# The first stage of a hybrid attention and state-space layer: x in half rows, the root's table fetched early, 1/rms taken with the scale, and another order of the first projection

## The chip, the cores and the metric

The program runs on one core of a Trainium2 chip. The metric is the time of one execution in device microseconds (us), as the median of the runs that are shown. The engines are TensorE (PE, with its weight loads as PEld), VectorE (DVE), ScalarE (ACT), GpSimd (POOL) and SyncE (SP), which issues the DMAs.

## What is computed

One layer of a diffusion backbone, in float32. Its first step is what matters here: the 512 rows of x are divided by their root mean square, scaled and shifted per column by two vectors that come from a matrix product with w_mod (the modulation), and multiplied by the columns of w_in. Seven blocks of 128 of these columns, called z, are made in the first stage; attention, the scan, the output projection and a last RMSNorm follow.

```python
shift, scale, gate = jnp.split((jax.nn.silu(c) @ w_mod + b_mod)[:, None, :], 3, axis=-1)
shift_c, scale_c, gate_c = jnp.split(jax.nn.silu(c_ctx) @ w_mod + b_mod, 3, axis=-1)
px = (rmsnorm(x, norm_g) * (1 + scale) + shift) @ w_in
pc = (rmsnorm(ctx, norm_g) * (1 + scale_c) + shift_c) @ w_in
...
y = xf * lax.rsqrt(jnp.mean(xf * xf, axis=-1, keepdims=True) + EPS)
```

## The kernel before, in words

Activations are held transposed: 16 blocks of 128 columns of x (`KT = 16`, index `j` or `k`), each a tile of 128 partitions by 512 tokens. For products in float32 quality each activation and each weight is split in a high part (a rounded copy, made by ScalarE) and a low part (what is left, made by a subtraction on VectorE or GpSimd), and every product is three matmuls: high by high, high by low, low by high.

**Loading x** (`load_latent`, lines 131 to 164). x comes in four column quarters, two DMAs each, with runs of 2 KB. For each quarter ScalarE squares the four token tiles with a sum along the row (line 145), and TensorE transposes 128 by 128 pieces into PSUM banks (line 150), four to a block. The block is copied out by VectorE, or by ScalarE for the last of each quarter (lines 151 to 154). Then the sums are reduced and scaled on VectorE (lines 155 and 103), the root is taken on ScalarE (line 104), which needs another activation table, its reciprocal and four diagonal matrices are made on VectorE (lines 105 and 160), TensorE spreads 1/rms over all partitions with them (line 161), and ScalarE copies the result to `rsb` (line 163).

**The blocks** (lines 216 to 254). For each block `j` four DMAs of 512 KB bring w_mod (`wm`, seven buffers), and 32 narrow matmuls make `md`, in four column groups of the array. ScalarE copies it (`mds`), four small matmuls sum the groups (`ms`), and VectorE adds the biases and makes `mv` (lines 241 and 242). `md` and `ms` lie in the one PSUM bank of tag `pv`, so the next block's `md` can't begin before VectorE has read `ms`. With `mv`, VectorE makes `full` from the normalised block (line 245), ScalarE the high part `xh` (line 247), VectorE the low part `xl` (line 249) and then the next block times 1/rms (`norm_x`, line 200). A DMA of 448 KB brings the weights of z (`wr`, three buffers; `wsr` in the trace), ScalarE casts them to `wh`, and GpSimd makes `wl` (lines 228 to 233). `z_part(j, us)` is the 21 z matmuls of a block, or some of them; those of block `j - 1` are put into block `j`: twelve between `md` and `ms`, nine behind `ms`.

**Order.** A planner lays out each engine's queue before the run: it goes through its own model of time, and gives each engine, of the instructions that are ready in it, the one that stands first in the code. On the chip each queue runs in that order. `keep_in_program_order` (all matmuls made with `mmo`, and `norm_x`) pins an instruction behind the one traced before it on its engine. `md` of block 0 is thus pinned behind the matmuls that spread 1/rms. SP's queue issues all DMAs here, in its own order, and waits there for a free buffer.

After the last block come the context's activations, v and dt (lines 255 to 394), and the rest of the layer.

Of the kernel before, what the change touches and what calls it, by code (L numbers as in the profile page):

```python
# [6 lines left out]
F32 = mybir.dt.float32  # L7
# [29 lines left out]
# columns of the packed constants  # L37
C_ID, C_SEL, C_AP, C_AN, C_TRI, C_TRIT, C_MF, C_MB, C_END = 0, 128, 130, 258, 386, 514, 642, 770, 898
# columns of the packed small parameters
# [4 lines left out]
def emit(tc, xin, ctxT, wmod, wgate, bgate, wz, wvd, wu, wo, fng, vecs, cst, rope, out, dbg=None):  # L44
# [15 lines left out]
    def f32(ap):  # L60
        return ap.bitcast(F32)

    with es:
# [12 lines left out]
        nc.sync.dma_start(c_sb, cst[:, 0:P + 2])  # L76
# [6 lines left out]
        identb = pc.tile([P, P], BF16, name="identb")  # L83
        nc.vector.tensor_copy(identb, ident)
# [3 lines left out]
        # persistent activations: transposed normalised inputs in two exact parts  # L88
        cy = es.enter_context(tc.tile_pool(name="cy", bufs=1))
        px_s = es.enter_context(ExitStack())  # L90
        px = px_s.enter_context(tc.tile_pool(name="px", bufs=1, side="right"))
        xh = [px.tile([P, S], F32R, tag=f"xh{k}", name=f"xh{k}") for k in range(KT)]
# [14 lines left out]
        def silu2(src, o, tmp):  # L107
            """o = 2 * src * sigmoid(src) = src * (1 + tanh(src / 2))"""
            nc.scalar.activation(tmp, src, AF.Tanh, scale=0.5)
            nc.vector.scalar_tensor_tensor(out=o, in0=tmp, scalar=1.0, in1=src, op0=ALU.add, op1=ALU.mult)  # L110

# [4 lines left out]
        def rms_rows(o, acc, n, tag):  # L116
            """1 / rms of every token, on all partitions, from the sums of squares per partition."""
# [13 lines left out]
        def load_latent():  # L131
            """Latent tokens: transposed as they come, in column blocks; 1 / rms of every token on all partitions."""
            xtags = ["mm", "sa", "tp", "mm", "sa", "tp", "mm"]
            ssq = sp.tile([P, NT, 4], F32, tag="ssq", name="ssq_x")
            rs = sp.tile([P, NT], F32, tag="rs", name="rs_x")
            xin_v = xin.rearrange("(t p) d -> p t d", p=P)
            for q in range(4):
                xt = []
                for h2 in range(2):
                    x_ = cy.tile([P, 2, 512], F32, tag=f"{('ca', 'cb')[h2]}{q}", name=f"xt_{q}_{h2}")  # L140
                    nc.sync.dma_start(x_, xin_v[:, 2 * h2:2 * h2 + 2, q * 512:(q + 1) * 512])
                    xt += [x_[:, 0, :], x_[:, 1, :]]
                for t in range(NT):
                    junk = sp.tile([P, 512], BF16, tag="stmp", name=f"junk_{q}_{t}")
                    nc.scalar.activation(junk, xt[t], AF.Square, accum_out=ssq[:, t, q:q + 1])
                for i in range(4):
                    k = 4 * q + i
                    tps = bank(xtags[k % 7], f"xT_{k}")
                    for t in range(NT):
                        nc.tensor.transpose(tps[:, t * P:(t + 1) * P], xt[t][:, i * P:(i + 1) * P], ident)  # L150
                    if i == 3:
                        nc.scalar.activation(xr[k], tps, AF.Copy)
                    else:
                        nc.vector.tensor_copy(xr[k], tps)
# [22 lines left out]
        # silu of the two modulation vectors, zero-padded to one column group  # L177
# [21 lines left out]
        def norm_x(j):  # L199
            tc.keep_in_program_order(nc.vector.tensor_tensor(out=xr[j], in0=xr[j], in1=rsb, op=ALU.mult))  # L200

        norm_x(0)

# [12 lines left out]
        for j in range(KT):  # L216
            mt = bank("pv", f"md_{j}", shape=(P, 260))
# [15 lines left out]
            tt(nc.gpsimd, wl, wr, f32(wh), ALU.subtract)  # L233
            wzs.append((wh, wl))
            if j > 0:
                z_part(j - 1, range(0, 4))
# [8 lines left out]
            nc.vector.tensor_scalar(out=full, in0=xr[j], scalar1=mv[:, 2:3], scalar2=mv[:, 0:1],  # L245
                                    op0=ALU.mult, op1=ALU.add)
            nc.scalar.activation(xh[j], full, AF.Copy)
            lo = px.tile([P, S], F32R, tag=f"xl{j}", name=f"xl{j}")
            tt(nc.vector, lo, full, f32(xh[j]), ALU.subtract)
            xl.append(lo)  # L250
            if j + 1 < KT:
                norm_x(j + 1)
            if j > 0:
                z_part(j - 1, range(4, NZ))
# [19 lines left out]
        def gate_step(ld):  # L274
            """One k block of 512 gate columns: products per partition, summed over partitions after the last."""
# [22 lines left out]
        def load_unit(u, ctxp=False):  # L298
            """Yields (k, hi, lo) weight blocks [128, 128] of unit u."""
# [110 lines left out]
        # dt: softplus(u) = max(u,0) + log1p(exp(-|u|)), log1p(e) = 2 atanh(e / (2 + e))  # L410
# [48 lines left out]
        def conv_silu(pa, pb, ci, o):  # L459
            """Depthwise conv of width 3 and silu: pa [128, n] in PSUM -> o in SBUF."""  # L460
# [13 lines left out]
        def ssd_group(g, units):  # L474
# [65 lines left out]
            for pr in range(2):  # L540
                tix = 2 * g + pr
                # state term of both heads at once: exp(cs) scales it afterwards
# [10 lines left out]
                for hh in range(2):  # L553
# [3 lines left out]
                    for d in range(2):  # L557
                        # the row of running sums on all partitions; the differences take its place
# [451 lines left out]
```

## Time and profile before

| | us |
|---|---|
| median of three runs | 1057.65 |
| lowest and highest | 1056.16 and 1060.71 |
| span of the profiled execution | 1054.8 |
| TensorE busy in it | 1009.6 (96%) |
| VectorE busy | 722.0 (68%) |
| ScalarE busy | 494.6 (47%) |
| GpSimd busy | 173.5 (16%) |

The share of an engine is an average over the whole span. Rows of the timeline give a start in us from the span's start, a duration, the engine, the line of the kernel, the operation, its output and inputs by the program's names with their shapes, how many were merged in the row, and in brackets how long the engine had been idle before it and what released it. A matmul's duration includes its way through the array, so that rows of matmuls that follow each other overlap; the distance between their starts is what each costs. The granted clock (PEclk) is 1.00 at TensorE's upper level of 2.4 GHz and 0.50 at the lower one of 1.2.

### The profile page before, as it was taken

To read this page: it belongs to the slowest core of one execution; us is meant where nothing else is said; L and a number is where in the kernel's file an instruction comes from. 1 tells how busy PE (TensorE), PEld (TensorE's weight loads), DVE (VectorE), ACT (ScalarE), POOL (GpSimd) and SP (SyncE) were. 2 spreads that over 40 slices of the span, in tenths; PEclk is the share of its full clock that TensorE was granted. 3 is DMA by queue.
4 is the path that set the end of the run, shared out by engine and by line. 5 is a ranking of instruction groups with operands and counts; after the bars stand their busy time and mean duration, and the time that the engine had idled before them with its cause. 6 is when DMAs were issued, how large, how long until landed. Compare 5 with 4: busy or idle time off the path is not lost.

```text
span 1054.8 us, 15524 instructions
## 1 busy us (share of the span) xinstructions
PE 1009.6 (96%) x5682; PEld 818.7 (78%) x5682; DVE 722.0 (68%) x1474; ACT 494.6 (47%) x1064; POOL 173.5 (16%) x120
## 2 busy tenths in 40 slices
PE   5999999999999989989989999999999998999996
PEld 4677789788778868868868777777777777888885
DVE  4332378585875985885889888788798866333765
ACT  6222275263352453263345567666666655333333
POOL 1232200000210110110037100000000008744220
PEclk9999999999999999989999999999999999999998
DMA  9999963354244244444331211112111135442304
GB/s 333 385 347 348 343 212 95 110 165 147 70 120 145 92 149 125 112 120 139 120 107 56 84 61 42 59 40 80 41 40 61 61 99 221 151 167 91 100 33 160
DMA packets 50845, 143.25 MB, mean 136 GB/s; under 512 B 5544, under 2 KB 5928, under 8 KB 50512
## 3 DMA queue, kind: packets, MB, share of 16 engines
q1 hardware_dynamic: 50768, 142.25, 40.5%
q8 instruction: 45, 0.74, 0.3%
q14 instruction: 32, 0.26, 0.1%
HBM read 137.96 MB, written 4.27 MB: 135 GB/s over the span
## 4 chain that ended last, share of the span: by engine, by line
PE 61%; DVE 12%; DMA 5%; ACT 3%; issue 3%; POOL 1%; SPq 0%; ACTq 0%; DVEq 0%; POOLq 0%
PE pj L49 25%; PE o L49 14%; PE pjc L49 5%; PE pv L49 3%; PE ptp L756 3%; PE sl L49 3%; DMA wg<-in_wgate_dram 2%; PE vps L49 2%; DVE df L566 2%; DVE wl L55 2%; DMA df<-csd 2%; PE sc L49 2%; DVE ga L290 1%; DVE df L575 1%; PE stx L49 1%
## 5 line engine op out<-in xcount | busy, mean ns | idle before, releaser
L49 PE MATMUL pj<-xh,wh 128*128 128x512 f32 x560 | 225.5, 403 | 0.0
L49 PE MATMUL pj<-xl,wh 128*128 128x512 f32 x560 | 224.6, 401 | 0.0
L49 PE MATMUL pj<-xh,wl 128*128 128x512 f32 x560 | 224.0, 400 | 0.0
L308 ACT ACTIVATE wh<-wr 128x512 fp32r<-128x512 f32 x140 | 87.9, 630 | 137.5 <-PE pjc L49 66.2
L49 PEld LDWEIGHTS pj<-xh,wl 128*128 128x128 f32 x560 | 105.7, 189 | 21.3 <-issue 0.9
L55 DVE TENSOR_TENSOR wl<-wr,wh 128x512 fp32r<-128x512 f32 x140 | 103.5, 742 | 24.9 <-ACT wh L308 21.0
L49 PEld LDWEIGHTS pj<-xl,wh 128*128 128x128 f32 x560 | 106.4, 190 | 15.1 <-issue 1.9
L49 PEld LDWEIGHTS pj<-xh,wh 128*128 128x128 f32 x560 | 106.5, 190 | 13.9 <-issue 1.0
L55 DVE TENSOR_TENSOR wol<-wo,woh 128x512 fp32r<-128x512 f32 x56 | 53.3, 968 | 63.6 <-ACT woh L846 57.3
L290 DVE SCALAR_TENSOR_TENSOR ga<-wg,sc,ga 128x512 f32<-128x512 f32 x64 | 50.8, 794 | 49.2 <-DMA wg<-in_wgate_dram 48.1
L55 POOL TENSOR_TENSOR ec<-ec,ec 128x512 f32<-128x512 f32 x8 | 11.2, 1397 | 349.2 <-DVE ec L55 328.9
L846 ACT ACTIVATE woh<-wo 128x512 fp32r<-128x512 f32 x56 | 34.8, 630 | 70.8 <-PE o L49 62.3
L55 POOL TENSOR_TENSOR hacc<-hacc,hsq 128x512 f32<-128x512 f32 x14 | 20.4, 1454 | 288.7 <-ACT hsq L654 286.3
L49 PE MATMUL pjc<-chq,wh 128*128 128x256 f32 x224 | 65.2, 291 | 2.1 <-DVE xs L468 2.1
L49 PE MATMUL pjc<-clq,wh 128*128 128x256 f32 x224 | 64.4, 288 | 0.0
L49 PE MATMUL pjc<-chq,wl 128*128 128x256 f32 x224 | 63.7, 284 | 0.0
L760 ACT ACTIVATE ph<-ptp 128x512 fp32r<-128x512 f32 x72 | 41.1, 597 | 28.2 <-PE ptp L756 26.8
L49 PE MATMUL o<-woh,hsh 128*128 128x512 f32 x128 | 50.9, 397 | 3.1 <-ACT part L865 3.1
L55 DVE TENSOR_TENSOR pl<-ptp,ph 128x512 fp32r<-128x512 f32 x72 | 48.4, 683 | 7.8 <-ACT ph L760 7.4
L566 DVE SCALAR_TENSOR_TENSOR df<-df,cs,cs_sb 128x128 f32<-128x128 f32 x128 | 48.3, 433 | 4.6 <-ACT ec L563 4.5
L49 PEld LDWEIGHTS pjc<-chq,wh 128*128 128x128 f32 x224 | 42.2, 189 | 11.5 <-ACT ec L563 1.6
L55 POOL TENSOR_TENSOR wsl<-wsr,wsh 128x896 fp32r<-128x896 f32 x16 | 33.9, 2116 | 101.0 <-ACT wsh L231 95.7
(282 smaller groups left out, 2341.8 us busy)
## 6 DMA issues: line engine op xcount, KB each, us to landing
wr<-in_wu_dram SPq DMA_DIRECT2D x70, 512.0 KB, 3.9
wm<-in_wmod_dram SPq DMA_DIRECT2D x64, 512.0 KB, 7.5
wg<-in_wgate_dram SPq DMA_DIRECT2D x64, 256.0 KB, 2.6
wo<-in_wo_dram SPq DMA_DIRECT2D x32, 512.0 KB, 4.5
df<-csd SPq DMA_DIRECT2D x32, 256.0 KB, 4.1
wsr<-in_wz_dram SPq DMA_DIRECT2D x16, 448.0 KB, 6.6
wr_v<-in_wvd_dram SPq DMA_DIRECT2D x16, 288.0 KB, 2.9
xt<-in_xin_dram SPq DMA_DIRECT2D x8, 512.0 KB, 7.5
```

The lines of the kernel that those rows point to most:

```text
L49: return nc.tensor.matmul(o, l, r, start=start, stop=stop)
L55: eng.tensor_tensor(out=o, in0=a, in1=b, op=op)
L290: geng.scalar_tensor_tensor(out=ga, in0=wg, scalar=sc0[:, k:k + 1], in1=ga, op0=ALU.mult, op1=ALU.add)
L308: nc.scalar.activation(wh, rr, AF.Copy)
L566: nc.vector.scalar_tensor_tensor(out=df[:, cc], in0=bc[:, cc], scalar=cs[:, d, c, r:r + 1], in1=mF if d == 0 else mB, op0=ALU.subtract, op ...
L575: nc.vector.scalar_tensor_tensor(out=dx[0][:, cc], in0=df[:, cc], scalar=dtt[:, d, c, r:r + 1], in1=dx[0][:, cc], op0=ALU.mult, op1=ALU.add)
L756: nc.tensor.transpose(tp[:, i * P:(i + 1) * P], pt[i][:, n * P:(n + 1) * P], ident)
L760: nc.scalar.activation(ph, tp, AF.Copy)
L846: nc.scalar.activation(wh, wr[:, i, :], AF.Copy)
```

## The change

- x comes in two column halves of four DMAs each, one for every token tile, with runs of 4 KB; the constants' DMA goes behind the first two. Each tile is squared at once over 1024 columns, eight squares in all. VectorE copies every transposed block.
- A root of one element stands ahead of the squares, so that its table is fetched there.
- `norm_x` is gone. `full` is the block times the scale times 1/rms, the shift goes into the making of the high part (as a bias) and of the low part.
- The low part of z's weights is made by VectorE.
- Four of block 0's seven groups of z products (twelve matmuls) go ahead of the modulation of block one, two groups between it and its sums, one behind.

Only comments differ elsewhere.

```diff
-        nc.sync.dma_start(c_sb, cst[:, 0:P + 2])
...
+        xt = [[cy.tile([P, 1024], F32, tag=f"{('ca', 'cb')[h2]}{t}", name=f"xt_{h2}_{t}") for t in range(NT)] for h2 in range(2)]
+        for h2 in range(2):
+            for t in range(NT):
+                nc.sync.dma_start(xt[h2][t], xin[t * P:(t + 1) * P, h2 * 1024:(h2 + 1) * 1024])
+                if (h2, t) == (0, 1):
+                    nc.sync.dma_start(c_sb, cst[:, 0:P + 2])
...
-            ssq = sp.tile([P, NT, 4], F32, tag="ssq", name="ssq_x")
+            ssq = sp.tile([P, NT, 2], F32, tag="ssq", name="ssq_x")
             rs = sp.tile([P, NT], F32, tag="rs", name="rs_x")
-            xin_v = xin.rearrange("(t p) d -> p t d", p=P)
-            for q in range(4):
-                xt = []
-                for h2 in range(2):
-                    x_ = cy.tile([P, 2, 512], F32, tag=f"{('ca', 'cb')[h2]}{q}", name=f"xt_{q}_{h2}")
-                    nc.sync.dma_start(x_, xin_v[:, 2 * h2:2 * h2 + 2, q * 512:(q + 1) * 512])
-                    xt += [x_[:, 0, :], x_[:, 1, :]]
+
+            nc.scalar.activation(rs[0:1, 0:1], expa[0:1, 0:1], AF.Sqrt)
+            for h2 in range(2):
                 for t in range(NT):
-                    junk = sp.tile([P, 512], BF16, tag="stmp", name=f"junk_{q}_{t}")
-                    nc.scalar.activation(junk, xt[t], AF.Square, accum_out=ssq[:, t, q:q + 1])
-                for i in range(4):
-                    k = 4 * q + i
+                    junk = sp.tile([P, 1024], BF16, tag="stmp", name=f"junk_{h2}_{t}")
+                    nc.scalar.activation(junk, xt[h2][t], AF.Square, accum_out=ssq[:, t, h2:h2 + 1])
+                for i in range(8):
+                    k = 8 * h2 + i
                     tps = bank(xtags[k % 7], f"xT_{k}")
                     for t in range(NT):
-                        nc.tensor.transpose(tps[:, t * P:(t + 1) * P], xt[t][:, i * P:(i + 1) * P], ident)
-                    if i == 3:
-                        nc.scalar.activation(xr[k], tps, AF.Copy)
-                    else:
-                        nc.vector.tensor_copy(xr[k], tps)
+                        nc.tensor.transpose(tps[:, t * P:(t + 1) * P], xt[h2][t][:, i * P:(i + 1) * P], ident)
+                    nc.vector.tensor_copy(xr[k], tps)
...
-        def norm_x(j):
-            tc.keep_in_program_order(nc.vector.tensor_tensor(out=xr[j], in0=xr[j], in1=rsb, op=ALU.mult))
-
-        norm_x(0)
...
         for j in range(KT):
+            if j == 1:
+                z_part(0, range(0, 4))
...
-            tt(nc.gpsimd, wl, wr, f32(wh), ALU.subtract)
+            tt(nc.vector, wl, wr, f32(wh), ALU.subtract)
             wzs.append((wh, wl))
             if j > 0:
-                z_part(j - 1, range(0, 4))
+                z_part(j - 1, range(4, 6) if j == 1 else range(0, 4))
...
-            nc.vector.tensor_scalar(out=full, in0=xr[j], scalar1=mv[:, 2:3], scalar2=mv[:, 0:1],
-                                    op0=ALU.mult, op1=ALU.add)
-            nc.scalar.activation(xh[j], full, AF.Copy)
+            nc.vector.scalar_tensor_tensor(out=full, in0=xr[j], scalar=mv[:, 2:3], in1=rsb, op0=ALU.mult, op1=ALU.mult)
+            nc.scalar.activation(xh[j], full, AF.Identity, bias=mv[:, 0:1])
             lo = px.tile([P, S], F32R, tag=f"xl{j}", name=f"xl{j}")
-            tt(nc.vector, lo, full, f32(xh[j]), ALU.subtract)
+            nc.vector.scalar_tensor_tensor(out=lo, in0=full, scalar=mv[:, 0:1], in1=f32(xh[j]), op0=ALU.add, op1=ALU.subtract)
             xl.append(lo)
-            if j + 1 < KT:
-                norm_x(j + 1)
             if j > 0:
-                z_part(j - 1, range(4, NZ))
+                z_part(j - 1, range(6 if j == 1 else 4, NZ))
```

## Rows read from the trace of the kernel before

**Rows 1.** Windows by stage: length, busy time of each engine, granted clock, DMA share, GB/s.

```profile
27.60:130.75 103.15, 103.14 (x800) 73.73 (x800) 32.27 (x72) 26.73 (x43) 29.64 (x14) 1.00 0.97 356
```

**Rows 2.** Timeline of one block in the steady part of the stage.

```profile
93.91 1.93 PE L49 MATMUL md<-wm,scp 128*32 128x256 f32 x32
...
95.77 0.51 PE L49 MATMUL zps<-xh,wsh 128*128 128x512 f32 x1
...
98.65 0.51 PE L49 MATMUL md<-c_sb,mds 128*128 128x2 f32 x4
...
99.26 0.22 DVE L241 TENSOR_SCALAR mv<-md,v_sb 128x2 f32<-128x2 f32 x1 [4.38 <-PE md L49]
...
101.28 1.93 PE L49 MATMUL md<-wm,scp 128*32 128x256 f32 x32
```

**Rows 3.** Waits of SP's queue up to 150 us: us in total, times, longest.

```profile
SPq L221 <- PE md L49: 72.8, 30, 6.6
```

**Rows 4.** Timeline from the last tile of x to modulation block 0.

```profile
16.04 1.09 PE L150 MATMUL xT<-c_sb,xt 128*128 128x128 f32 x8 [0.17 <-DMA xt<-in_xin_dram]
...
16.52 1.89 DVE L154 COPY xr<-xT 128x512 f32<-128x512 f32 x3 [0.81 <-PE xT L150]
...
18.62 0.17 DVE L155 TENSOR_REDUCE rs_x<-ssq_x 128x4 f32<-128x16 f32 x1 [0.22 <-ACT junk L145]
...
19.08 1.28 ACT L104 ACT_TABLE_LOAD   x1
20.38 0.20 ACT L104 ACTIVATE rs_x<-rs_x 128x4 f32<-128x4 f32 x1
...
21.26 1.56 PE L49 MATMUL rps<-dg,ones 128*128 128x128 f32 x8 [4.13 <-DVE dg L160]
...
22.76 3.11 PE L49 MATMUL md<-wm,scp 128*32 128x256 f32 x32
```

**Rows 5.** Timeline on to modulation block two.

```profile
26.38 0.61 PE L49 MATMUL md<-c_sb,mds 128*128 128x2 f32 x4 [0.51 <-ACT mds L227]
...
27.61 1.93 PE L49 MATMUL md<-wm,scp 128*32 128x256 f32 x32 [0.62 <-PE md L49]
28.12 0.63 ACT L247 ACTIVATE xh<-full 128x512 fp32r<-128x512 f32 x1 [1.79 <-DVE full L245]
...
28.78 0.69 DVE L55 TENSOR_TENSOR xl<-full,xh 128x512 fp32r<-128x512 f32 x1 [0.69 <-ACT xh L247]
...
34.97 1.93 PE L49 MATMUL md<-wm,scp 128*32 128x256 f32 x32
```

**Rows 6.** Groups by form: count, busy us, mean ns of one, idle before.

```profile
L145 ACT ACTIVATE junk<-xt 128x512 bf16<-128x512 f32 x16 | 9.9, 619 | 3.5 <-DMA xt<-in_xin_dram 3.5
...
L245 DVE TENSOR_SCALAR full<-xr,mv 128x512 f32<-128x512 f32 x15 | 8.2, 545 | 0.6
```

**Rows 7.** Windows of 2 us: with x's transfers, and at modulation block 0.

```profile
14.00:16.00 2.00, 1.51 (x13) 1.06 (x10) 1.71 (x3) 2.00 (x7) 0.00 (x0) 1.00 1.04 397
...
22.00:24.00 2.00, 2.00 (x16) 1.13 (x19) 0.51 (x1) 1.14 (x2) 0.00 (x0) 0.50 1.02 406
```

**Rows 8.** Groups by form up to 230 us: the context's Identity activations.

```profile
L379 ACT ACTIVATE chq<-fullc,mv 128x256 fp32r<-128x256 f32 x16 | 7.2, 499 | 2.4 <-DVE fullc L377 2.3
```

**Rows 9.** Timeline of the last block, and a wait of TensorE from 100 us on.

```profile
134.63 2.22 DVE L55 TENSOR_TENSOR wl_v<-wr_v,wh_v 128x576 fp32r<-128x576 f32 x1 [2.92 <-ACT wh_v L342]
...
PE zps L49 <- ACT xh L247: 0.2, 1, 0.2
```

**Rows 10.** The weights of z: issue and cast of one block, and the sixteen landings.

```profile
87.66 0.39 SPq L229 DMA_DIRECT2D wsr<-in_wz_dram  x1
...
96.25 0.94 ACT L231 ACTIVATE wsh<-wsr 128x896 fp32r<-128x896 f32 x1
...
DMA to landing us min/median/max: 5.6/6.6/8.3
```

**Rows 11.** Waits of TensorE from 100 us on: us in total, times, longest.

```profile
PE yps L49 <- DVE df L55: 13.6, 4, 4.0
```

More of the change, by code (lines that the diff above doesn't have):

```diff
@@ L81, in vec @@
             return v_sb[:, o + i:o + i + n]
-        identb = pc.tile([P, P], BF16, name="identb")
-        nc.vector.tensor_copy(identb, ident)
         ones = pc.tile([P, P], F32, name="ones")
@@ L91, in emit @@
         px = px_s.enter_context(tc.tile_pool(name="px", bufs=1, side="right"))
+        xt = [[cy.tile([P, 1024], F32, tag=f"{('ca', 'cb')[h2]}{t}", name=f"xt_{h2}_{t}") for t in range(NT)] for h2 in range(2)]
[4 more added lines that the diff above has]
+                    nc.sync.dma_start(c_sb, cst[:, 0:P + 2])
+        identb = pc.tile([P, P], BF16, name="identb")
+        nc.vector.tensor_copy(identb, ident)
         xh = [px.tile([P, S], F32R, tag=f"xh{k}", name=f"xh{k}") for k in range(KT)]
```

## The prediction

> **What bounds the kernel now.** I read the windows by stage first. From 27.6 to 130.75 us TensorE is busy for 103.14 of 103.15 us at the full granted clock [rows 1]. DMA is at 0.97 in the same stretch, so the next view must say which of the two leads. The timeline of one block says TensorE: the 32 modulation products of one block start at 93.91 and those of the next at 101.28, a period of 7.37 us, with products end to end between them [rows 2]. The waits of SP's queue say the same: it waits 72.8 us in 30 times for modulation products to give their buffers back [rows 3]. A block moves 2.56 MB, which at the 397 to 406 GB/s of the busiest windows takes 6.4 us [rows 7]. DMA therefore has about 1 us to spare in each block, and what counts in this stage is when TensorE's unbroken run begins. It begins with the modulation of block one (blocks counted from 0; the title's "block two" is this one) at 27.61, and the second follows at 34.97 [rows 5]. Everything after shifts with that point. So the whole change is priced at one place: when do block two's modulation products start, against 34.97.
>
> Ahead of that stands a chain through four engines [rows 4]: the last tile of x lands and is transposed at 16.04, three copies on VectorE run from 16.52, the sum of squares is reduced at 18.62, a table is loaded from 19.08, the root runs at 20.38, its spread over partitions on TensorE at 21.26, and modulation block 0 at 22.76. Those products keep TensorE's order, so 1/rms gates them although they don't read it.
>
> **The change part by part.**
>
> **Half rows.** Runs of 4 KB replace runs of 2 KB. The window with x moves 397 GB/s and one with w_mod alone, which has 4 KB runs, 406 [rows 7]: 2% of the 14 us in which x comes is 0.3 us. Bounds are 0 and 1.3 us (one tile of 0.52 MB at 397 GB/s, should the later start of w_mod leave the queues to x). I take -0.3, the row at hand.
>
> The other face of half rows is what is left to do after the last tile. Before, a quarter of the columns: four blocks, three copied by VectorE and one by ScalarE. After, half of the columns: eight blocks, all copied by VectorE. Three copies took 1.89 us [rows 4], so eight take 5.0 and end at 16.52 + 5.0 = 21.5. TensorE is no help or hindrance: eight transposes took 1.09 us. The reduction stands behind the copies in the code, and VectorE's queue is laid out in code order among what the planner sees ready; a copy is ready every 0.1 us and takes 0.63, so I put all eight first. The reduction then starts at 21.5 and not 18.62: **+2.9**. The lower bound is the first rival.
>
> **Eight squares for sixteen.** One of 512 columns takes 0.62 us [rows 6] and an ACTIVATE of 896 columns 0.94 [rows 10], so 1.05 at 1024. The last ends at about 16.04 + 1.05 + 0.2 = 17.3 and not 18.6. With the copies on VectorE until 21.5 this gain is hidden: 0.
>
> **The root's table.** The load began at 19.08, when the scaled sum was there, and the root at 20.38 [rows 4]. Without it the root begins where the load did: **-1.3**. The load now lies ahead of the first squares, while ScalarE waits for x. An Identity activation behind the same root table runs with no load of its own [rows 8], and the squares never had one either.
>
> The Trainium skill, ScalarE: Activation LUTs, section What ACT_TABLE_LOAD costs, gives 2.66 us for a switch, the load plus a drain of 1.38. The row shows the load alone: the root starts 0.02 us behind its end. By the page this term would be -2.66 and the sum 1.36 lower; the trace decides.
>
> So block 0's modulation starts at 22.76 - 0.3 + 2.9 - 1.3 = 24.06, **+1.3**. It ran for 3.11 us because the clock was granted at half in this stretch [rows 4, 7], where a later block takes 1.93; TensorE again idles ahead of it, so I leave 3.11.
>
> **First products ahead of modulation block one.** Before, that modulation started 27.61 - 22.76 = 4.85 us after block 0's, gated by the read of the shared PSUM bank. Now twelve z products stand ahead of it in a pinned order. The first needs xh, done 28.12 + 0.63 = 28.75, 5.99 after block 0's start; the second needs xl, done 28.78 + 0.69 = 29.47, 6.71 after [rows 5]. Both come 0.14 later, since the scale with 1/rms reads two tensors: 0.69, the two-tensor price of xl, against 0.55 [rows 5, 6]. A product is 2.88 / 12 = 0.24 us [rows 2], so the run counts from 6.85 - 0.24 = 6.61: **+1.76**. In return the wait for the data of block one is covered, but before there was none: products ran on from 27.61. Queued behind are the modulation of block one and all of TensorE.
>
> At the end of that block only three products, 0.72 us, stand between the four small column sums and block two's modulation, which waits until VectorE has read the bank; the way from sums to modulation took 27.61 - 26.38 = 1.23 [rows 5]. With 0.3 for the sums themselves **+0.2**, bounds 0 and 0.5.
>
> **1/rms with the scale.** Sixteen products of VectorE go (0.69 each, at no one's cost, behind 4.38 us of idle per block [rows 2]), and full grows by 0.14. Cover: the same idle time. Without it, the 0.14 per block would show.
>
> **The low half of the weights on VectorE.** On VectorE, 896 columns of two tensors cost between 0.69 (the 512-column price [rows 5]) and 1.4 (twice that); 1.2 by columns. It fits in the 4.38 us of idle in each block: 0 in the steady part. In the last block a VectorE split met GpSimd's and took 2.22 us; TensorE then waited 0.2 for xh [rows 9]. That goes: **-0.2**. The new wait, VectorE's queue behind the weights' landing, is the second rival. In block 0 this split and ScalarE's cast of the same weights could stand ahead of the root or of the diagonal: 0 to +1.4, taken at 0.
>
> **Sum.** 1.3 + 1.76 + 0.2 - 0.2 = +3.0 us. The profiled span of 1054.8 lies 2.85 under the median of the runs, so a profile of 1057.8 and a median of 1057.65 + 3.0 = **1060.7 us**. Own bounds: +2.0 (landing a tile earlier) to +4.7.
>
> **The rivals.**
>
> **The reduction gets in between the copies.** For it: the squares end at 17.3, four us ahead of the last copy, and if the planner took transposes as slower than copies there would be gaps. Against it: code order, and copies that are always ready. The reduction starts at about 17.9; from there to the spread 21.26 - 18.62 - 1.3 = 1.34, plus up to 1.8 for a copy ahead of each of three small steps: 18.9 to 21.0, middle 19.9, so -1.4. TensorE then idles about 2.5 us where it idled 4.1, so block 0's modulation may keep the full clock: -1.2. Then +1.76 and +0.2 stay, -0.2 and -0.3 too: -1.1, or 1056.5 (1055 to 1058).
>
> **VectorE waits for weights, slower by much.** The low half now stands in VectorE's queue ahead of the modulation's bank read, and TensorE waits for that read. Weights issued at 87.66 land after a median of 6.6, at 94.3; ScalarE's cast runs at 96.25 to 97.2, the split would end at 98.4, the read came at 99.26 and is needed by about 100.8 [rows 2, 10]. Slack: 1.95 + 2.4 = 4.3 us. It decides from a landing of 10.9 us; each us beyond costs 14 blocks one us each, so 0.5 beyond gives 1060.7 + 7 = 1068. Against it: the longest landing of the sixteen was 8.3 [rows 10], and DMA has time to spare.
>
> **The early table does nothing**, should the squares or the root load again: 1060.7 + 1.3 = 1062. Against it: rows 8.
>
> **Order elsewhere.** The planner's clock moves, so a later stage may be laid out otherwise. The longest single wait of TensorE there is 4.0 us [rows 11]: plus or minus 4.
>
> **How the numbers follow.** Forecast 0.58; reduction between the copies 0.26; VectorE waiting for weights 0.04; table 0.05; order elsewhere 0.07. The range reaches from the first rival's low end to just over the forecast's upper bound and the table case: 1054.5 to 1063. A measurement of this kernel tells about 0.5%, 5.3 us, from no change; forecast, first rival and table lie within: same 0.91. Slower by more: the weights' wait and half of a bad order, 0.07. Faster by more: 0.02.
>
> **What would show it.** Right: a reduction behind eight copies at about 21.5, no load ahead of the root, block 0's modulation near 24, a TensorE gap of about 2 us up to the first z product, block two's modulation near 38, then a period of 7.37. Wrong: a reduction before 19, a gap under 1 us ahead of the first product, block two's modulation before 35, a longer period, or a table load at the squares.

## The result, and the profile of the changed kernel

The changed kernel takes 1064.74 us (median of four runs, 1063.40 to 1069.05) beside 1058.44 for the kernel before (four runs): a ratio of 1.0066, interval 1.0039 to 1.0093. The forecast was 1060.7, range 1054.5 to 1063.0. So it is 4.0 us slower than forecast, and beyond the range.

The timeline of the changed kernel, from the second half's first copy to the modulation of block three (blocks are counted from 0, as in the prediction; start, duration, engine, line, operation; the bracket is the idle time before and what ended it):

```profile
18.12 4.87 DVE L153 COPY xr<-xT 128x512 f32<-128x512 f32 x8 [0.75 <-PE xT L152]
...
22.91 0.15 DVE L154 TENSOR_REDUCE rs_x<-ssq_x 128x4 f32<-128x8 f32 x1
...
23.30 0.20 ACT L110 ACTIVATE rs_x<-rs_x 128x4 f32<-128x4 f32 x1 [5.54 <-DVE rs_x L109]
...
24.18 2.05 PE L49 MATMUL rps<-dg,ones 128*128 128x128 f32 x8 [4.66 <-DVE dg L159]
...
26.16 3.64 PE L49 MATMUL md<-wm,scp 128*32 128x256 f32 x32
...
30.30 0.61 PE L49 MATMUL md<-c_sb,mds 128*128 128x2 f32 x4 [0.50 <-ACT mds L223]
...
32.25 0.72 ACT L242 ACTIVATE xh<-full,mv 128x512 fp32r<-128x512 f32 x1 [2.00 <-DVE full L241]
33.00 0.75 DVE L244 SCALAR_TENSOR_TENSOR xl<-full,mv,xh 128x512 fp32r<-128x512 f32 x1 [0.79 <-ACT xh L242]
...
33.02 0.69 PE L49 MATMUL zps<-xh,wsh 128*128 128x512 f32 x1 [2.11 <-ACT xh L242]
...
33.81 0.80 PE L49 MATMUL zps<-xl,wsh 128*128 128x512 f32 x1
...
37.82 1.93 PE L49 MATMUL md<-wm,scp 128*32 128x256 f32 x32
...
42.42 1.93 PE L49 MATMUL md<-wm,scp 128*32 128x256 f32 x32
...
49.84 1.93 PE L49 MATMUL md<-wm,scp 128*32 128x256 f32 x32
```

What the reader is to see, beside [rows 4, 5]: all eight copies stand ahead of the reduction, the root has no table load ahead of it, and the root's chain is short (22.91 to 24.18, 1.27 us, where it was 2.64). But modulation block 0 starts at 26.16 and takes 3.64 us (before 22.76 and 3.11), TensorE is idle for 2.11 us ahead of the first z product, and the modulation of block two starts at 42.42, not at 34.97: **+7.45 us**. The forecast had it near 38, +3.3 at this place (1.3 + 1.76 + 0.2; its total of +3.0 takes off 0.2 for the last block). From there the delay neither grows nor shrinks: the later block below starts its modulation at 101.36 and the next at 108.72, a period of 7.36 as in [rows 2], with the split of the weights on VectorE (1.09 us) done ahead of the bank's read.

```profile
97.32 1.09 DVE L55 TENSOR_TENSOR wsl<-wsr,wsh 128x896 fp32r<-128x896 f32 x1 [2.65 <-ACT wsh L227]
...
99.29 0.22 DVE L237 TENSOR_SCALAR mv<-md,v_sb 128x2 f32<-128x2 f32 x1 [0.88 <-PE md L49]
...
101.36 1.93 PE L49 MATMUL md<-wm,scp 128*32 128x256 f32 x32
...
108.72 1.93 PE L49 MATMUL md<-wm,scp 128*32 128x256 f32 x32
```

The windows of 2 us say why the first blocks are long (length, busy time of PE, PEld, DVE, ACT and POOL, then the clock granted to TensorE, DMA share, GB/s):

```profile
22.00:24.00 2.00, 0.00 (x0) 0.00 (x0) 1.66 (x7) 0.70 (x2) 0.00 (x0) 0.73 1.01 405
24.00:26.00 2.00, 1.82 (x8) 1.78 (x8) 1.62 (x5) 0.34 (x1) 0.00 (x0) 0.50 0.21 82
26.00:28.00 2.00, 2.00 (x22) 0.93 (x24) 0.00 (x0) 0.60 (x1) 0.00 (x0) 0.50 0.04 8
28.00:30.00 2.00, 1.80 (x20) 0.46 (x12) 0.00 (x0) 0.13 (x1) 0.00 (x0) 0.56 0.83 184
30.00:32.00 2.00, 0.61 (x4) 0.52 (x4) 0.94 (x3) 0.25 (x1) 0.00 (x0) 1.00 0.95 353
32.00:34.00 2.00, 0.87 (x2) 0.38 (x3) 1.12 (x3) 1.56 (x2) 0.00 (x0) 0.79 1.03 403
34.00:36.00 2.00, 2.00 (x5) 1.62 (x6) 0.94 (x1) 0.00 (x0) 0.00 (x0) 0.50 0.83 338
36.00:38.00 2.00, 2.00 (x11) 1.29 (x14) 0.00 (x0) 0.00 (x0) 0.00 (x0) 0.85 0.00 0
```

The clock is at its lower level (0.50, 1.2 GHz) twice. The first fall follows the idle 4.66 us ahead of the spread of 1/rms, as before [rows 7], and lasts through the spread and block 0's modulation. The second is new: it follows the idle 2.11 us ahead of the first z product. From the third on the z products stand 0.43 us apart until 36.54 and 0.23 to 0.26 after that, and the twelve take from 33.02 to 37.82, 4.80 us, where [rows 2] gave 2.88. DMA rests too (share 0.21 and 0.04 from 24 to 28), since the w_mod buffers come free with modulation (up to 45 us SP's queue waits 21.4 us for modulation products, in 7 times).

### The profile page after: what moved, and what is told of

Its sections match the earlier page's. It is cut to its first block, busy times and chain, and to the rows that moved or that the text cites. A ratio compares the mean times of both kernels' runs of the same rounds, so it can differ in the third digit from the quotient of the medians.

```text
span 1062.8 us, 15463 instructions
## 1 busy us (share of the span) xinstructions
PE 1015.9 (96%) x5682; PEld 821.9 (77%) x5682; DVE 735.4 (69%) x1478; ACT 492.3 (46%) x1045; POOL 140.9 (13%) x104
## 4 chain that ended last, share of the span: by engine, by line
PE 75%; DVE 13%; DMA 4%; ACT 3%; issue 2%; POOL 1%; SPq 0%; ACTq 0%; DVEq 0%; POOLq 0%
PE pj L49 26%; PE o L49 14%; PE zps L49 8%; PE pjc L49 5%; PE md L49 4%; PE pv L49 3%; PE vps L49 3%; PE ptp L749 3%; PE sl L49 3%; DMA wg<-in_wgate_dram 2%; DVE wl L55 2%; DVE df L559 2%; PE sc L49 2%; DVE ga L283 1%; DVE df L568 1%
## 5 line engine op out<-in xcount | busy, mean ns | idle before, releaser
L49 PEld LDWEIGHTS pj<-xh,wh 128*128 128x128 f32 x560 | 106.8, 191 | 13.9 <-issue 1.0
L49 PE MATMUL o<-wol,hsh 128*128 128x512 f32 x128 | 50.8, 397 | 0.0
```

The lines of the kernel that those rows point to most:

```text
L49: return nc.tensor.matmul(o, l, r, start=start, stop=stop)
```

## The experiments

Two theories. **Clock:** the part that the forecast lacks is TensorE at half speed behind the idle times that the change leaves on it. **Order:** it is the order of queues and of loading, with half rows landing late, copies ahead of the reduction and products behind xh, at whatever clock. To take out when x landed in an execution, most distances below go from VectorE's first copy of the last part of x (the second half, or the last quarter) to the modulation of block two: 24.30 us in the changed kernel, 18.45 in the kernel before (34.97 - 16.52). A ratio is always to the kernel before, in runs on the same chip.

### The z products back behind modulation block one

```diff
-            if j == 1:
-                z_part(0, range(0, 4))
...
-                z_part(j - 1, range(4, 6) if j == 1 else range(0, 4))
+                z_part(j - 1, range(0, 4))
...
-                z_part(j - 1, range(6 if j == 1 else 4, NZ))
+                z_part(j - 1, range(4, NZ))
```

> The changed kernel with the order of the first z products as it was before: the modulation of block one stands ahead of them again. Theory (the new order costs about 2 us of idle TensorE, and by that idle time keeps the granted clock low for longer): block 0's modulation stays at 26.2 us, block one's starts about 31.6 and not 37.8, block two's at 39 to 40.5 and not 42.4; span 2 to 3.5 us under the changed kernel's 1062.8. Rival (the new order only covers the landing of block one's weights, which come late here because their buffer is freed late): block one's modulation stretches over the wait, block two's stays within 0.5 us of 42.4 and the span within 1.

Ratio 1.0006 (0.9987 to 1.0026). Timeline:

```profile
16.59 4.87 DVE L153 COPY xr<-xT 128x512 f32<-128x512 f32 x8 [0.75 <-PE xT L152]
...
24.63 2.82 PE L49 MATMUL md<-wm,scp 128*32 128x256 f32 x32
...
29.19 1.93 PE L49 MATMUL md<-wm,scp 128*32 128x256 f32 x32 [0.62 <-PE md L49]
...
36.73 1.93 PE L49 MATMUL md<-wm,scp 128*32 128x256 f32 x32
```

From the copy to block two it is 20.14 us: 4.16 less than in the changed kernel. Block two comes at 36.73, where 39 to 40.5 was expected; 1.53 us of that is the earlier start of the copies, the rest a larger gain. Not all of the 4.16 belongs to the z products: modulation block 0 stands ahead of them in both kernels, and it took 2.82 us here and 3.64 there. From its end to block two it is 9.28 us here, and 12.62 and 13.98 in the two traces of the changed kernel, so z ahead cost 3.3 and 4.7 us. The forecast priced it at 1.96 (1.76 and 0.2). What is left over the kernel before, 20.14 - 18.45 = 1.69, is the other parts: eight copies for three (4.79 to the reduction where it was 2.10, +2.69), the chain from reduction to spread (1.27 for 2.64, -1.37), the slower spread (1.98 for 1.50, +0.48), and -0.11. So this one part is more than half of the loss, and 1.7 to 2.4 times its price.

### TensorE kept busy with filler products

Products of the identity with itself, into a bank that nobody reads, ahead of the spread (22 of them) and ahead of the first z product (6). Their results are not used; all else is the changed kernel.

```diff
+            busy = bank("pv", "busy", shape=(P, P))
+            for _ in range(22):
+                mmo(busy, ident, ident, True, True)
             rps = bank("tp", "rps")
...
             if j == 1:
+                for _ in range(6):
+                    mmo(md[:, 0:P], ident, ident, True, True)
                 z_part(0, range(0, 4))
```

> The changed kernel with 22 products of the identity with itself in TensorE's idle time ahead of the spread of 1/rms, and six more ahead of the first z product; their results are not used. Theory (part of the loss is the granted clock, at half from about 24 to 36.5 us in the changed kernel): the clock stays at the upper level, block 0's modulation takes about 1.9 us and not 3.6, the twelve z products about 2.9 and not 4.8, block two's modulation starts 2 to 3.5 us before 42.4, the span falls by as much. Rival (waits for other engines set these starts, the clock is hidden): block two's modulation within 0.7 us of 42.4.

Ratio 1.0016 (1.0000 to 1.0033), with more work than the changed kernel. The copies start at 16.59, and the granted clock is 1.00 in every window from 20 to 40 us. Timeline, and two windows:

```profile
22.74 1.06 PE L50 MATMUL rps<-dg,ones 128*128 128x128 f32 x8
...
23.72 1.93 PE L50 MATMUL md<-wm,scp 128*32 128x256 f32 x32
...
28.88 0.50 PE L50 MATMUL zps<-xh,wsh 128*128 128x512 f32 x1
...
32.41 1.93 PE L50 MATMUL md<-wm,scp 128*32 128x256 f32 x32
...
37.02 1.93 PE L50 MATMUL md<-wm,scp 128*32 128x256 f32 x32
```

```profile
22.00:24.00 2.00, 2.00 (x25) 1.79 (x27) 1.05 (x5) 0.17 (x1) 0.00 (x0) 1.00 1.02 397
...
28.00:30.00 2.00, 1.71 (x11) 1.24 (x10) 0.82 (x2) 0.98 (x2) 0.00 (x0) 1.00 1.00 371
```

The order is that of the changed kernel, product for product, and the distance falls from 24.30 to 20.43: 3.87 us of the stage were the clock (4.94 beside the second trace of the changed kernel, below). Block two comes 5.40 us sooner, where 2 to 3.5 was expected; 1.53 of it is again the start. From the end of modulation 0 to block two it is 11.37 us here, and 9.28 where z stands behind (the kernel above, at the full clock from there on): the order itself costs 2.1, near the forecast's 1.96. The twelve z products take 3.53 us at the full clock and not 2.88, because the second waits for xl. Both theories hold a part, and this run parts them. Of the 3.3 and 4.7 us that z ahead cost, 2.1 are order and 1.2 and 2.6 the clock. The rest of the 3.87 is spread and modulation 0, which take 2.91 us here and 5.62 in the first trace of the changed kernel.

### The reduction ahead of the second half's copies

The squares, the reduction, the root and the diagonals are written ahead of the second half's copies in the code.

```diff
+            squares(0)
+            blocks(0)
+            squares(1)
+            nc.vector.tensor_reduce(out=rs, in_=ssq, axis=AX.X, op=ALU.add)
+            rstd_of(rs, rs, D)
...
+            blocks(1)
             rps = bank("tp", "rps")
```

> The changed kernel with the reduction, root and diagonals written ahead of the copies of the second half, so that VectorE's queue has them between the third and the seventh of its eight copies; nothing else changes. Theory (the eight copies ahead of the reduction set 1/rms): the spread over partitions starts at 21.5 to 22.5 and not 24.2, block 0's modulation about 2 us sooner, block two's 2 to 4.5 us sooner (the upper end if TensorE's shorter idle time also keeps the clock). Rival (the transposes or the landing of x set it): the spread starts within 0.5 us of 24.2.

Ratio 1.0021 (1.0005 to 1.0038). Timeline, and the windows behind it:

```profile
17.29 1.29 DVE L155 COPY xr<-xT 128x512 f32<-128x512 f32 x2 [0.75 <-PE xT L154]
...
18.49 0.15 DVE L160 TENSOR_REDUCE rs_x<-ssq_x 128x4 f32<-128x8 f32 x1
...
20.91 1.95 PE L49 MATMUL rps<-dg,ones 128*128 128x128 f32 x8 [2.22 <-DVE dg L165]
...
22.79 2.72 PE L49 MATMUL md<-wm,scp 128*32 128x256 f32 x32
...
39.41 1.93 PE L49 MATMUL md<-wm,scp 128*32 128x256 f32 x32
```

```profile
28.00:30.00 2.00, 1.14 (x2) 0.63 (x3) 1.60 (x2) 0.69 (x1) 0.00 (x0) 0.50 0.97 229
...
32.00:34.00 2.00, 2.00 (x6) 1.61 (x5) 0.00 (x0) 0.00 (x0) 0.00 (x0) 0.50 0.62 252
```

The reduction gets in behind two copies, and modulation 0 comes 5.50 us behind the first copy and not 8.04. The spread starts 3.62 us behind the copy where it was 6.06, 2.44 sooner (expected 1.7 to 2.7). That is the forecast's first rival, made here by an edit, and its gain of 2.54 at modulation 0 is about the 2.7 by which the forecast set the two apart (-1.4 against +1.3). But idle time ahead of the spread is still 2.22 us, and the clock was at half through modulation 0 all the same: the rival's -1.2 for a kept clock was wrong. Then the z products run at half for all twelve (28.74 to 34.65, 5.91 us), and of 2.54 gained at modulation 0, 2.18 are left at block two.

### The constants loaded ahead of x

In the changed kernel the first transpose waits for the identity: the timeline's row for it reads

```profile
9.02 5.74 PE L152 MATMUL xT<-c_sb,xt 128*128 128x128 f32 x34 [9.02 <-DMA c_sb<-in_cst_dram]
...
15.03 1.04 PE L152 MATMUL xT<-c_sb,xt 128*128 128x128 f32 x6 [0.27 <-DVE xr L153]
```

where before it was 6.37, waiting for x. This run puts the constants back ahead of x.

```diff
         nc.sync.dma_start(v_sb, vecs)
+        nc.sync.dma_start(c_sb, cst[:, 0:P + 2])
...
-                if (h2, t) == (0, 1):
-                    nc.sync.dma_start(c_sb, cst[:, 0:P + 2])
```

> The changed kernel with the constants' DMA in its old place, ahead of x. Theory (the identity comes at 8.9 us behind two tiles of x, so the first half's transposes and copies are late, hold the PSUM banks, and make the second half late): transposes start at about 7.5 and not 9.0, the second half's first copy at 17.0 to 17.5 and not 18.1, block two's modulation 0.6 to 1.2 us sooner. Rival (the last tile's landing sets the second half): its first copy stays within 0.3 us of 18.1.

Ratio 1.0052 (1.0026 to 1.0077): nothing is gained that can be measured. Transposes begin at 6.71, but the first copy only at 11.63 (it needs a transpose from each of the four tiles, and TensorE runs without a gap until then). The second half's first copy comes at 17.26. That lies in the expected 17.0 to 17.5, but it doesn't show the theory: in two kernels above that have the constants behind two tiles (z behind, fillers) this copy came at 16.59. From there to block two it is 24.04, as in the changed kernel (24.30). In every kernel with half rows the second half's first copy follows the first half's by 5.62 or 5.63 us, the eight copies (4.87) and 0.75, whenever the last tile lands: the second row above shows transposes of the second half (34 stand ahead of them, and the first half has 32) that wait for a copy of the first half to free a bank, and TensorE takes its transposes in order. In the changed kernel ScalarE squares the last tile from 16.61, so it had landed 1.5 us ahead of that copy.

### Z ahead alone, in the kernel before

```diff
         for j in range(KT):
+            if j == 1:
+                z_part(0, range(0, 4))
...
-                z_part(j - 1, range(0, 4))
+                z_part(j - 1, range(4, 6) if j == 1 else range(0, 4))
...
-                z_part(j - 1, range(4, NZ))
+                z_part(j - 1, range(6 if j == 1 else 4, NZ))
```

> The kernel before with the new order of the first z products alone. Theory (it costs idle time ahead of the first product, and the idle time lets the clock fall a second time): block 0's modulation to block two's, 12.2 us before, grows by 2 us if the clock stays up and by up to 5 if it falls, so 14.2 to 17; the runs come out 2 to 5 us over the kernel before. Rival (the loss needs the late start of the changed kernel; here the products fill a wait): within 1 us of 12.2, runs within 1 us.

Ratio 1.0019 (1.0005 to 1.0032). Timeline:

```profile
23.10 2.80 PE L49 MATMUL md<-wm,scp 128*32 128x256 f32 x32
...
28.83 0.79 PE L49 MATMUL zps<-xh,wsh 128*128 128x512 f32 x1 [1.81 <-ACT xh L249]
...
39.43 1.93 PE L49 MATMUL md<-wm,scp 128*32 128x256 f32 x32
```

Modulation 0 to two is 16.33 us, 4.1 more than the 12.21 of [rows 4, 5], without half rows or anything else of the change, and 4.4 more from the end of modulation 0 (13.53 and 9.10). TensorE is idle for 1.81 us, then the clock is at half from 28.83 (0.50 in the windows from 30 to 34). All of it lies in the expected range. The cost of this part is its own, and again over twice its price.

### The early table alone, in the kernel before

```diff
+            nc.scalar.activation(rs[0:1, 0:1], expa[0:1, 0:1], AF.Sqrt)
             for q in range(4):
```

> The kernel before with the early root alone, so that its table is fetched ahead of the last squares. Theory (the load stands alone on the chain): from the reduction to the spread of 1/rms 1.3 us and not 2.64, block two's modulation 1.3 us sooner after the last tile's copies (17.1 us behind their first and not 18.45). Rival of the notes (a load with a drain of 1.4 us goes): 2.7 us sooner. Rival (squares reload their own table): no sooner.

Ratio 0.9982 (0.9966 to 0.9997). Timeline:

```profile
19.11 0.17 DVE L156 TENSOR_REDUCE rs_x<-ssq_x 128x4 f32<-128x16 f32 x1 [0.66 <-ACT junk L146]
...
20.41 1.64 PE L49 MATMUL rps<-dg,ones 128*128 128x128 f32 x8 [3.22 <-DVE dg L161]
...
26.39 2.10 POOL L55 TENSOR_TENSOR wsl<-wsr,wsh 128x896 fp32r<-128x896 f32 x1 [24.99 <-ACT wsh L232]
26.69 2.08 DVE L246 TENSOR_SCALAR full<-xr,mv 128x512 f32<-128x512 f32 x1
```

Reduction to spread is 1.30 us where it was 2.64 [rows 4]: -1.34 for a forecast of -1.3. The Trainium skill, ScalarE: Activation LUTs, What ACT_TABLE_LOAD costs, gives 2.66 us for a switch of tables with its drain. The trace doesn't agree: little more than the load's own 1.28 comes back. Ahead of the reduction VectorE waits 0.66 us for ScalarE's squares, which with quarters end last; [rows 4] had 0.22, and the kernel below, without the early table, 0.48, so little of that is the table's. In the changed kernel the load stands behind the first square (8.57 us), where eight squares of 1.04 us have time to spare. Block two's modulation was expected 17.1 us behind the first copy and came 18.91 behind it, at 35.48, later than before, because GpSimd's split of the weights met the making of `full`, which took 2.08 us and not 0.55 [rows 6].

### The scale with 1/rms, and the split on VectorE, in the kernel before

```diff
-            tt(nc.gpsimd, wl, wr, f32(wh), ALU.subtract)
+            tt(nc.vector, wl, wr, f32(wh), ALU.subtract)
...
-            if j + 1 < KT:
-                norm_x(j + 1)
```

with `full`, `xh` and `xl` as in the change.

> The kernel before with two parts: 1/rms taken with the scale, and the low half of z's weights on VectorE instead of GpSimd. Theory (both lie beside TensorE's work): the period of a block stays at 7.36 to 7.37 us, block two's modulation is 0 to 0.3 us later behind the last tile's copies, the read of the sums in the last block, 136.77 before, comes 0.6 to 0.8 us sooner for the same start; runs within 1 us of the kernel before. Rival (VectorE's queue now waits for weights and TensorE for VectorE): a period over 7.4 us and runs 1 us or more later.

Ratio 0.9990 (0.9971 to 1.0010). The period is 7.37 (35.77 to 43.14), and the read of the sums in the last block comes at 136.82, 0.75 us sooner for the same start, as expected. Both cover terms of the forecast were right: `full` and `xl` take 0.75 us and `xh` 0.72, and the steady part doesn't notice. One part missed: block two comes 19.29 us behind the first copy, 0.84 later than before, where 0 to 0.3 was expected. Of this, 0.26 is a reduction that waited longer for ScalarE's squares, and 0.48 the spread, 1.98 us for 1.50, with the clock at 0.50 in the window from 20 to 22 where it was 0.95 before.

### Modulation block 0 ahead of the spread, in the kernel before

If 1/rms gates modulation only by its place in TensorE's queue, modulation can go first and fill the idle time. With quarters, the early table, the scale and the split on VectorE, z behind:

```diff
+            def spread():
+                rps = bank("tp", "rps")
+                for t in range(NT):
+                    mmo(rps[:, t * P:(t + 1) * P], ones, dgs[t], True, True)
+                nc.scalar.activation(rsb, rps, AF.Copy)
+            return rsb, spread
...
+            if j == 0:
+                spread()
             mds = su.tile([P, 256], F32, tag="mds", name=f"mds_{j}")
```

> The kernel before (x in quarters, copies shared with ScalarE, z products in the old order) with the early table, 1/rms with the scale, the low half of the weights on VectorE, and one new thing: the modulation of block 0 stands ahead of the spread of 1/rms on TensorE, since it doesn't read 1/rms. Theory (1/rms gated block 0's modulation by its place in the queue only, and TensorE's idle time with the clock went with it): block 0's modulation runs from 17 to 20.5, as its weights land, block two's starts at 30.5 to 33, 2 to 4.5 us sooner, then the landing of weights binds for some blocks; runs 1.5 to 4 us under the kernel before. Rival (weights land too late for that): block two's modulation within 1 us of 34.97.

Ratio 0.9984 (0.9966 to 1.0001). Timeline:

```profile
17.77 0.64 PE L49 MATMUL md<-wm,scp 128*32 128x256 f32 x8 [0.28 <-DMA wm<-in_wmod_dram]
...
21.53 0.64 PE L49 MATMUL md<-wm,scp 128*32 128x256 f32 x8 [0.66 <-DMA wm<-in_wmod_dram]
...
22.10 1.16 PE L49 MATMUL rps<-dg,ones 128*128 128x128 f32 x8
...
27.81 0.64 PE L49 MATMUL md<-wm,scp 128*32 128x256 f32 x8 [0.65 <-DMA wm<-in_wmod_dram]
...
33.87 1.93 PE L49 MATMUL md<-wm,scp 128*32 128x256 f32 x32
```

The clock stays at 1.00 without a filler, and block two comes 17.00 us behind the copy, 1.45 sooner than before. The early table is in this kernel too, so the run doesn't show how much of that the new place of modulation 0 gives alone. At 33.87 block two is later than the expected 30.5 to 33: the four pieces of modulation 0 now wait for the landing of their weights, and those of block one too. The stage's start has become DMA's, and the rival, weights that land too late, was nearly right.

### The changed kernel again, and fillers in the kernel before

The first is the changed kernel as it is, measured and profiled a second time.

> The changed kernel once more, unchanged, with more runs. Theory (the loss is 24.3 us from the second half's first copy to block two's modulation against 18.5 before, less under 1 us in the last block; the landing of the first tiles moves by 1 to 1.5 us between executions and added to it in the first profile): the distance is again 24 to 24.6 us, block two's modulation starts between 40.5 and 42.5 with the landing, the runs lie 5 us over the kernel before, a ratio of 1.004 to 1.006. Rival (the late landing belongs to the half rows): the second half's first copy is again near 18.1 and the ratio 1.0066.

Ratio 1.0093 (1.0072 to 1.0113), where 1.004 to 1.006 was expected. Timeline:

```profile
31.37 0.80 PE L49 MATMUL zps<-xh,wsh 128*128 128x512 f32 x1 [2.11 <-ACT xh L242]
...
42.12 1.93 PE L49 MATMUL md<-wm,scp 128*32 128x256 f32 x32
```

The copies start at 16.75, only 0.23 later than before, yet block two's modulation is at 42.12: 25.37 us from the copy, over the expected 24 to 24.6. The late start of the first trace (18.12) was that execution's; the loss is not. All twelve z products ran at half speed here, 5.78 us from the first to block one's modulation. What follows for the theory of late landing: over the seven traces with half rows the copies start at 16.59 to 18.12, mean 17.08; over the six with quarters at 16.48 to 16.87, mean 16.65. So the landing with half rows gains nothing here and may cost 0.4 us, and it is not the cause. The copies that half rows leave behind the last tile are another matter, +2.69.

The second puts 16 filler products, whose results are not used, ahead of the spread in the kernel before.

```diff
+            busy = bank("pv", "busy", shape=(P, P))
+            for _ in range(16):
+                mmo(busy, ident, ident, True, True)
             rps = bank("tp", "rps")
```

> The kernel before with 16 products of the identity in TensorE's idle time ahead of the spread of 1/rms, results not used. Theory (the half clock costs the kernel before too, and the changed kernel more): the clock stays up, the spread to the modulation takes about 1.0 us and not 1.5, block 0's modulation 1.93 and not 3.11, block two's modulation starts 1.5 us sooner behind the last tile's copies; runs 0 to 2 us under the kernel before. Rival (the clock is covered by waits): block two's modulation unmoved.

Ratio 1.0012 (0.9992 to 1.0032), where 0 to 2 us less than before was expected. Modulation 0 takes 1.93 us and the spread 1.06 to it, where [rows 4] had 3.11 and 1.50; block two comes 17.35 us behind the copy, 1.10 sooner (expected 1.5). Block one's modulation then waits 0.64 us for weights. So the kernel before already lost 1.6 us to the clock (4.61 less 2.99), and DMA takes part of it when it is given back.

### The changed kernel mended

The reduction early, z behind, constants first, modulation 0 ahead of the spread: the edits above together, on the changed kernel.

> The changed kernel with its three faults mended: the reduction written ahead of the second half's copies, the z products in the old order, the constants first, and block 0's modulation ahead of the spread of 1/rms. Theory (nothing else in the change costs time, and then the landing of the weights binds): TensorE's clock stays up from the first block on, block two's modulation starts at 33 to 34.5, as in the kernel with x in quarters and the modulation first; runs 0 to 3 us under the kernel before. Rival (half rows cost by themselves): block two's modulation 1 us or more later than 34.5.

Ratio 1.0014 (0.9997 to 1.0030). Timeline:

```profile
33.13 1.93 PE L49 MATMUL md<-wm,scp 128*32 128x256 f32 x32
```

The clock is 1.00 in every window from 18 to 42 us, and block two's modulation is the earliest of all, as expected: 1.84 us ahead of the kernel before and 9.3 ahead of the changed kernel. But the time is not 0 to 3 us below the kernel before's, as was expected with it. The lowest version here, the early table alone, is at 0.9982, and its interval ends at 0.9997; among this many comparisons that is too little to say that it beats the kernel before.

## Does the end follow block two?

The forecast priced the whole change at one place, block two's start. Twelve measurements of eleven kernels test that. The second column is the start in the profiled execution less 34.97; the third is the ratio less one, times 1058 us, and its intervals reach 1.4 to 2.9 us to either side.

| kernel | block two, us | time, us |
|---|---|---|
| changed | +7.45 | +7.0 |
| changed, again | +7.15 | +9.8 |
| constants first | +6.33 | +5.5 |
| z ahead alone | +4.46 | +2.0 |
| reduction early | +4.44 | +2.2 |
| changed, fillers | +2.05 | +1.7 |
| changed, z behind | +1.76 | +0.6 |
| scale and split alone | +0.80 | -1.1 |
| table alone | +0.51 | -1.9 |
| before, fillers | -1.01 | +1.3 |
| modulation 0 first | -1.10 | -1.7 |
| changed, mended | -1.84 | +1.5 |

Only roughly. Where block two moved by 4.4 us or more, the time came out 2.0 us or more later; between -1.9 and +2.1 the two columns don't follow each other, and they differ by up to 3.3 us. The traces show where they part. In all thirteen, the first product of v on TensorE starts 102.9 to 103.1 us behind block two's modulation, so the start is carried whole through the blocks. From there to the end the kernel before needs 916.8 us, and the others between 1.6 less and 4.2 more. So the rest arises late. TensorE's waits in the scan and attention stay much as they were (those of [rows 11] come to 13.9 us in the changed kernel and 13.6 before), but the clock falls in some of them and not in others. Summed over windows of 2 us from 200 to 1045 us, 1 less the granted clock, times 2 us, comes to 6.8 us in the kernel before, 12.0 and 11.9 in the two traces of the changed kernel, 8.6 with z behind, 5.1 and 5.2 with the table or z alone, 10.2 in the mended one and 13.6 with modulation 0 first. These sums go with the late part only loosely: the changed kernel has 12.0 in the trace whose late part is 0.6 us longer than the kernel before's, and 11.9 in the one where it is 4.2 longer. Whether a kernel has such losses by its nature or an execution by chance, one or two traces of each can't say: it stays open.

## Why the prediction was wrong, step by step

- **What bounds the stage, and where to price it:** right for the stage. The period is 7.37 before and 7.36 after, and block two's start is carried whole through the blocks. That everything after shifts with it held only roughly.
- **Landing, -0.3:** wrong in sign, and in kind. The second half's copies start by the first half's (5.63 us behind), not by the last tile. Mean +0.4; +1.6 in the first trace, +0.2 in the second.
- **Eight copies ahead of the reduction, +2.9:** right, +2.69, and in the order said.
- **Table, -1.3:** right, -1.37. The rival that it does nothing falls.
- **Block 0's modulation at its 3.11 us:** this step failed. "TensorE again idles ahead of it, so I leave 3.11" took the clock for a constant of the place. Spread and modulation went from 4.61 (1.50 and 3.11) to 5.62 (1.98 and 3.64) in the first trace and 5.3 in the second. With z behind the same products took 4.80, and at the full clock 2.91, so this size changes with the execution.
- **z ahead, +1.76 and +0.2:** here the same step failed by most. The order was sized rightly, 2.1 at the full clock. But the twelve products were priced at the 0.24 us of the steady part, though the text itself forecast a gap of some 2 us ahead of them. The gap came (2.11), the clock was at half behind it, and the twelve took 4.80 and 5.78 us, where they take 3.53 at the full clock. So z ahead cost 3.3 and 4.7 us in the changed kernel and 4.4 in the kernel before.
- **1/rms with the scale, split on VectorE:** right, 0 in the steady part; the rival that VectorE waits for weights did not come. TensorE's wait of 0.2 us for xh in the last block [rows 9] is gone.
- **The rival with the reduction between the copies:** it did not happen by itself; made by an edit, its time to modulation was right and its kept clock was not. Its earliest spread, 18.9, should be 19.2 by its own terms (17.9 and 1.34).

The sum for the first trace, in us: start of the copies +1.60, copies +2.69, root's chain -1.37, order of z +2.1, clock +2.3 (3.87 in the changed kernel less the 1.6 that the kernel before already lost), 0.1 unexplained: +7.45. For the second: start +0.23, copies +2.69, chain -1.37, order +2.1, clock +3.3 (0.7 in spread and modulation 0, 2.6 in the z products), 0.2 unexplained: +7.15. The forecast's +3.3 at this place lacks the start (1.9 with its sign in the first trace, 0.5 in the second, so chance for the most part) and the clock (2.3 and 3.3). It had all the rows for the clock: [rows 7] shows what an idle TensorE gets, and the first rival even gave the clock a price in the other direction. It was not asked of the gap that the change makes.

## What to carry to other kernels

When an edit makes TensorE wait for even a few microseconds, price the products behind the gap at the lower clock as well as the upper, in the sum and not as a rival: here what stood behind gaps of 4.7 and 2.1 us ran 3.9 us longer for it. Work that needs none of what the engine waits for (here modulation ahead of 1/rms) belongs into the gap, and pinning products that need late data ahead of products that need none does the opposite. And time such an edit by a distance inside its stage, because here the later stages moved the end by 1.6 us less to 4.2 us more of their own.

## What the runs showed of the hardware that was not expected

- Behind an unfilled gap of 1.8 to 2.1 us ahead of the first z product the clock was at the lower level in all five traces that have it (four kernels). Between modulation 0 and that gap TensorE ran only the four small sums (0.61 us in all). With the gap filled by six small products, and the gap ahead of the spread by 22, the clock was 1.00. Behind a gap of 2.22 us ahead of the spread it was 0.50 too (from 22 to 24), while pieces of modulation with 0.3 to 0.7 us between them kept 1.00.
- `full` on VectorE took 2.08 us beside GpSimd's split and not 0.55. It began 0.30 us behind it and ended 0.28 behind its end. The Trainium skill, SBUF — State Buffer, SBUF: two separate sides, has GpSimd and VectorE's operations of certain kinds take one shared pair of ports in turn, each for a whole instruction. That VectorE waited agrees; with its own 0.55 behind the other's end it would have ended 0.27 later than it did, and the spans on GpSimd are rough.
- An operation on VectorE with two tensors and a scalar took 0.75 us for 512 columns where the one with two tensors took 0.69, and ScalarE's activation with a bias 0.72 where the copy took 0.63 [rows 5].
